# A hybrid attention and pooling block: W_out's quarter sums prepared early, loaded into attention's buffers, and later products begun inside the last heads

## The chip, the cores and the metric

The kernel is one launch on one core of a Trainium2 chip. A core has a matrix engine (PE, whose weight loads are listed apart as PEld), a vector engine (DVE), a scalar or activation engine (ACT), a general engine (POOL), and a sync engine (SP) whose queue issues every DMA of this kernel. The engines run side by side and wait for each other by semaphores; each executes its own instructions in the order in which the built program lists them. The metric is the time of the launch in microseconds; lower is better.

## The reference

The input x is 4096 tokens by 1024 channels, float32, with one conditioning vector c:

```python
mod = c @ w_ada + b_ada                      # 3072 numbers
shift, scale, gate = split(mod, 3)
h = rms_norm(x, norm_g) * (1 + scale) + shift
proj = h @ w_in                              # q|k|v|u|z: 512+512+512+512+1024
q, k = rms_norm(q, q_norm_g), rms_norm(k, k_norm_g)   # per head of 64
a_out = chunk_attention(q, k, v, rel_bias)   # 8 heads; a chunk of 64 tokens sees itself and 8 chunks to its left
p_out = multiscale_pool(u, w_pool, pool_scale)        # trailing means over 2, 4, 8, 16 frames
y = concat(a_out, p_out) * silu(z)
out = x + gate * (y @ w_out)                 # w_out is 1024 x 1024
```

## The kernel before

Every float32 product on PE is made of three matmuls: each operand is split into a rounded part `hi` and a rest `lo` (`split`, L101: ACT rounds, another engine subtracts), and hi·hi, hi·lo and lo·hi are summed in PSUM.

**The first stage** (pools `a_*`, L150 to L419) runs over eight groups of 512 tokens (`sg`). A group makes twelve products `n` of 24 matmuls each: gates of the pool half (`zp`), gates of the attention half (`za`), and the pooled channels `u`. Products with odd `n` go into one of two PSUM tiles `ps`, those with even `n` into one of four tiles `aps`, and `evac` (L325) empties them: for a gate ACT takes a sigmoid and DVE multiplies by the product. While a group runs, `load_x` fetches the next group's tokens, takes the root of their mean square, and sends it to DRAM and back as a row (`rs_d`, L200, and `rb`, L202); `prep` (L278) multiplies the transposed tokens by that row on POOL (L284), scales and shifts them on DVE (L285), and splits them. The normalised tokens are kept in `hT_d`, the gates in `gz_d`, the finished pool half of y in `yT_d`. At the end of the last group the 1024 numbers of `gate` are made (`ada`, eight times) and stored in `gate_d`.

**Attention** (L502 to L808) runs over 64 units: two passes of four heads, in each eight groups of 512 tokens, in each four heads. `s1_items` makes scores for one unit ahead (four blocks of 128 queries: PE, then DVE adds the bias and takes the extreme, then ACT takes the exponential); `s2_items` transposes the weights through PE and multiplies them by v. `proj_items` makes q, k and v of one block of 128 tokens for later units; its `evac_qk` squares q and k on POOL, sums on DVE, and takes eight reciprocal roots (`rsqrt`: three small DVE operations, then twelve small ones on POOL). `merge` interleaves these lists, and a scheduler that knows estimated durations then sets the final order of each engine's instructions.

**The output product** multiplies y (two blocks of 128 tokens at a time: block p and block p+16, p from 0 to 15, and the halves of the channels) by w_out with a scheme of seven block products per p. Two of the seven, w_out's two quarters in the first output half applied to block p, are `osteps`: 32 steps of 12 matmuls (`o_items`, L475). 24 of them (plan, L756) are handed to the units 58 to 63; the scheduler lays two more there. Their weights are loaded and split at u == 57 (`load_wo`). The other five products per p (`steps`, L850; called t = 2, 1, 3, 4, 0) use sums and differences of w_out's quarters. They begin when attention is over and its pools have been closed: `w_prep` (L833) loads w_out's quarters, forms the sums on DVE and POOL and splits them; `combine` (L864) forms sums and differences of y's blocks on POOL; `step` (L879) does 12 matmuls; the results are multiplied by `gate` on DVE and x is added on POOL (`finish`, L446).

Of the kernel before, what the change touches and what calls it, by code (L numbers as in the profile page):

```python
# [51 lines left out]
def block_kernel(ctx, tc, x, xT, par, crow, w_adaT, w_in, w_uT, bias, w_pool, w_out, rcnt, out):  # L52
# [17 lines left out]
    gate_d = dram.tile([1, D], F32, name="gate_d")  # L70
    s1_d = [dram.tile([P, SG], F32, name=f"s1_d{i}") for i in range(NPAIR)]
# [4 lines left out]
    nc.sync.dma_start(pt, par)  # L76

# [4 lines left out]
    def rsqrt(pool, src, n, inv_n, tag, eng=None):  # L82
# [3 lines left out]
        nc.vector.tensor_scalar(v, src, inv_n, EPS, op0=ALU.mult, op1=ALU.add)  # L86
# [63 lines left out]
    with ExitStack() as ca:  # L150
# [54 lines left out]
        mod = const.tile([P, 24], F32, name="mod")  # L205
        gcol = const.tile([P, KT], F32, name="gcol")
        psc = pt[:, C_PS : C_PS + 4]
        cb = wc.tile([P, D + 16], F32, name="cb")
        nc.gpsimd.memset(cb[:, D : D + 1], 1.0)

        def ada(pool, n):
            m = mod[:, n : n + 1]
            e = D if pool is xp else D + 1
            s_ = pool.tile([P, D if pool is xp else D + 16], F32, name="xt" if pool is xp else "w_s")[:, 0:e]
# [171 lines left out]
        nc.sync.dma_start(rc, rcnt)  # L386
        halo = [wc.tile([P, 16], F32, name=f"halo{g}") for g in range(4)]
# [3 lines left out]
        for sg in range(NSG):  # L391
            nxt = sg + 1 < NSG
            for n in range(12):
# [14 lines left out]
                evac(sg, n, ps)  # L408
                if not nxt and n == 3:
# [6 lines left out]
            if not nxt:  # L416
                for j in range(8):
                    ada(xp, 16 + j)
                nc.sync.dma_start(gate_d.rearrange("o (j p) -> p (o j)", p=P), mod[:, 16:24])  # L419


    op = ctx.enter_context(tc.tile_pool(name="b_qk", bufs=8))
    WO = {}
    gate = {}

    def load_wo(n, j, pool, stage):
        a_ = pool.tile([P, 2, 512], F32R, name="w")
        b_ = pool.tile([P, 2, 512], F32R, name="w")
        for t in range(2):
            s_ = stage()  # L430
            nc.sync.dma_start(s_, wo[:, 2 * j + t, n * 512 : n * 512 + 512])
            split(a_[:, t, :], b_[:, t, :], s_, nc.gpsimd)
            WO[n, 2 * j + t] = (a_[:, t, :], b_[:, t, :])
# [4 lines left out]

    def product(ps, a_, l_, W, start):
        for k in range(4):  # L440
            wh, wl = W[k]
            nc.tensor.matmul(ps, a_[:, k, :], wh, start=start and k == 0, stop=False, skip_group_check=True)  # L442
            nc.tensor.matmul(ps, a_[:, k, :], wl, start=False, stop=False, skip_group_check=True)  # L443
            nc.tensor.matmul(ps, l_[:, k, :], wh, start=False, stop=k == 3, skip_group_check=True)  # L444

    def finish(c, n, xr, b, eng):  # L446

        nc.vector.tensor_tensor(c, c, gate[n], op=ALU.mult)
        eng.tensor_tensor(c, c, xr, op=ALU.add)
        nc.sync.dma_start(out[b * P : (b + 1) * P, n * 512 : (n + 1) * 512], c)  # L450
# [13 lines left out]
    def o_load(i):  # L464
        if i < len(osteps):
# [9 lines left out]
    def o_items(i):  # L475
        half, p = osteps[i]

        def one(k):
# [4 lines left out]
            wh, wl = WO[0, half * 4 + k]  # L483
# [3 lines left out]
            if k == 3:  # L487
                OH.pop(i)
                o_load(i + 2)
                t = op.tile([P, 512], F32, name="qkr")  # L490
                if half == 0:
                    nc.scalar.copy(t, ps)
                    nc.sync.dma_start(s1_d[p], t)
                else:
                    nc.vector.tensor_tensor(t, ps, gate[0], op=ALU.mult)
                    nc.gpsimd.tensor_tensor(t, t, xr, op=ALU.add)
                    nc.sync.dma_start(out[p * P : (p + 1) * P, 0:512], t)
# [4 lines left out]
    with ExitStack() as cb:  # L502
# [21 lines left out]
        gqn = bp.tile([P, 1], F32, name="gqn")  # L524
# [19 lines left out]
        Vt, QK, QS, QL = {}, {}, {}, {}  # L544

        def proj_items(ph, b, after=None):
# [20 lines left out]
            def evac_qk(ps):  # L567
# [4 lines left out]
                ssq = st.tile([P, 8], F32, name="ssq")  # L572
                nc.vector.tensor_reduce(ssq, sq.rearrange("p (a b) -> p a b", b=HD), axis=AX.X, op=ALU.add)
                r = rsqrt(st, ssq, 8, 1.0 / HD, "rq", nc.gpsimd)
                r3 = raw.rearrange("p (a b) -> p a b", b=HD)
                nc.gpsimd.tensor_tensor(r3, r3, r.unsqueeze(2).broadcast_to([P, 8, HD]), op=ALU.mult)
                QK[ph, b] = raw

# [162 lines left out]

        units = [(ph, sg, h) for ph in range(2) for sg in range(NSG) for h in range(HP)]
# [13 lines left out]
        for i in range(24):  # L756
            plan[58 + i // 4].append(("o", i))
# [3 lines left out]
        def block_items(kb):  # L761
            if kb[0] == "o":
                return o_items(kb[1])
            it = proj_items(*kb, after=after.get(kb))
# [14 lines left out]
        for u in range(-1, 64):  # L779
# [21 lines left out]
            if u == 57:  # L801
                for n in range(2):
                    gate[n] = bp.tile([P, 512], F32, name=f"gate{n}")
                    nc.sync.dma_start(gate[n], gate_d[:, n * 512 : (n + 1) * 512].broadcast_to([P, 512]))
                for j in range(KT // 2):
                    load_wo(0, j, w1, stage)
                for j in range(2, 4):
                    load_wo(1, j, w1, stage)  # L808

    with ExitStack() as cd:  # L810
# [156 lines left out]
```

## Time and profile before

| | |
|---|---|
| runs | 1951.62, 1954.4, 1955.83 us; median 1954.4 |
| profiled execution | 1953.81 us, of which the span of the trace is 1952.0 |
| busy share | PE 97%, DVE 64%, POOL 49%, ACT 47% |
| matmuls | 10284 |
| DMA | 239.96 MB, mean 123 GB/s |

The page's table of 40 slices (48.8 us each) gives the busy share in tenths: PE stands at 9 or more in all but three of them (7 in the first, 6 and 7 in the 35th and 36th), and the granted clock of PE falls below 9 tenths only in the first, the 35th and the 36th. A matmul's listed duration overlaps that of the next, so pace is read from starts.

### The profile page before, as it was taken

How to read it: one execution, taken by the hardware profiler on the slowest of the kernel's cores; microseconds unless marked ns; L12 is line 12 of the kernel's file. 1: busy time of each engine (PE TensorE's matmuls, PEld its weight loads, DVE VectorE, ACT ScalarE, POOL GpSimd, SP SyncE). 2: the span in 40 equal slices, each digit the busy share in tenths (PEclk: the TensorE clock that was granted, in tenths of full speed). 3: DMA queues.
4: the chain of work that ended last, by engine and by line, in shares of the span. 5: the costliest groups of instructions: out<-in, count | busy, mean ns of one | idle time of the engine just before them, and what ended most of it. 6: DMA issues, size and time to landing. Idle time of an engine off the chain costs nothing. (4 is left out here: it accounts for less than half of the span.)

```text
span 1952.0 us, 30102 instructions
## 1 busy us (share of the span) xinstructions
PE 1890.8 (97%) x10284; PEld 1621.8 (83%) x10284; DVE 1247.7 (64%) x2456; ACT 913.4 (47%) x1951; POOL 948.3 (49%) x1449
## 2 busy tenths in 40 slices
PE   7999999999999999999999999999999999679998
PEld 6878888888888898898888888888898888568887
DVE  7664645464654557666676766657666654678896
ACT  4422212221324557656676666656666765422221
POOL 2431323132136653464565556544464654587774
PEclk8999999999999999999999999999999999889999
DMA  9654435434532222221233222112221455656664
GB/s 367 201 170 137 128 120 160 125 111 150 157 111 68 68 68 65 61 71 55 71 100 96 74 84 82 60 55 68 64 71 58 149 181 171 203 166 206 219 208 137
DMA packets 185066, 239.96 MB, mean 123 GB/s; under 512 B 20688, under 2 KB 96976, under 8 KB 184912
## 3 DMA queue, kind: packets, MB, share of 16 engines
q1 hardware_dynamic: 184912, 238.04, 38.1%
q8 instruction: 81, 1.33, 0.3%
q14 instruction: 73, 0.60, 0.1%
HBM read 166.53 MB, written 63.06 MB: 118 GB/s over the span
## 5 line engine op out<-in xcount | busy, mean ns | idle before, releaser
L556 PE MATMUL ps<-w,bhh 128*128 128x512 f32 (+1 forms) x1024 | 352.4, 344 | 0.3 <-ACT qkr L569 0.2
L557 PE MATMUL ps<-w,bhh 128*128 128x512 f32 (+1 forms) x1024 | 351.7, 343 | 0.0
L558 PE MATMUL ps<-w,bhl 128*128 128x512 f32 (+1 forms) x1024 | 350.9, 343 | 0.0
L699 DVE TENSOR_TENSOR ptl<-ptps,pth 128x512 fp32r<-128x512 f32 x480 | 224.1, 485 | 136.0 <-ACT pth L698 131.9
L103 POOL TENSOR_TENSOR bhl<-bhr,bhh 128x512 fp32r<-128x512 f32 x148 | 191.8, 1298 | 175.8 <-ACT bhh L102 157.2
L649 DVE CUSTOM_DVE_ANT_0 p<-sps,nb 128x640 f32<-128x640 f32 (+4 forms) x256 | 198.9, 777 | 115.7 <-PE sps L645 113.6
L662 ACT ACTIVATE p<-p,mx 128x640 f32<-128x640 f32 (+4 forms) x256 | 204.7, 800 | 101.7 <-DVE mx L649 100.6
L698 ACT CAST pth<-ptps 128x512 fp32r<-128x512 f32 x480 | 193.5, 426 | 124.2 <-PE ptps L692 111.8
L692 PE MATMUL ptps<-ident,p 128*128 128x128 f32 x1200 | 215.2, 275 | 1.6 <-ACT p L662 1.0
L556 PEld LDWEIGHTS ps<-w,bhh 128*128 128x128 f32 x1024 | 193.6, 189 | 18.2 <-DVE v L103 0.6
L558 PEld LDWEIGHTS ps<-w,bhl 128*128 128x128 f32 x1024 | 193.5, 189 | 17.7
L557 PEld LDWEIGHTS ps<-w,bhh 128*128 128x128 f32 x1024 | 193.6, 189 | 17.3
L710 PE MATMUL ops<-pth,v 128*128 128x512 f32 x480 | 162.1, 338 | 5.7 <-ACT pth L698 2.8
L692 PEld LDWEIGHTS ptps<-ident,p 128*128 128x128 f32 x1200 | 147.9, 141 | 21.1 <-ACT p L662 1.7
L644 PE MATMUL sps<-kr,qs 128*128 128x320 f32 (+2 forms) x480 | 154.8, 330 | 8.3 <-DVE mx L649 7.5
L711 PE MATMUL ops<-ptl,v 128*128 128x512 f32 x480 | 156.6, 335 | 2.9 <-DVE ptl L699 2.0
L322 PE MATMUL aps<-hlo,w 128*128 128x512 f32 x392 | 154.0, 393 | 0.0
L323 PE MATMUL aps<-hhi,w 128*128 128x512 f32 x392 | 152.5, 389 | 0.0
L321 PE MATMUL aps<-hhi,w 128*128 128x512 f32 x392 | 150.5, 394 | 0.0
L645 PE MATMUL sps<-kr,ql 128*128 128x320 f32 (+2 forms) x480 | 149.1, 319 | 0.0
L321 PE MATMUL ps<-hhi,w 128*128 128x512 f32 x376 | 147.5, 396 | 1.0 <-DVE gz L330 1.0
L322 PE MATMUL ps<-hlo,w 128*128 128x512 f32 x376 | 147.9, 393 | 0.0
(176 smaller groups left out, 4166.8 us busy)
## 6 DMA issues: line engine op xcount, KB each, us to landing
bhr<-hT_d SPq DMA_DIRECT2D x128, 256.0 KB
xt<-in_x_dram SPq DMA_DIRECT2D x32, 512.0 KB
qkr<-in_x_dram SPq DMA_DIRECT2D x64, 256.0 KB
dr<-yT_d SPq DMA_DIRECT2D x64, 256.0 KB
xt<-in_xT_dram SPq DMA_DIRECT2D x28, 512.0 KB
hT_d<-xt SPq DMA_DIRECT2D x56, 256.0 KB
w_s<-in_w_adaT_dram SPq DMA_DIRECT2D x16, 512.5 KB
gz_d<-gz SPq DMA_DIRECT2D x32, 256.0 KB
```

The source lines that it names most:

```text
L103: eng.tensor_tensor(lo, raw, hi.bitcast(F32), op=ALU.subtract)
L321: nc.tensor.matmul(ps, wh[:, cs], a_, start=k == 0, stop=False)
L322: nc.tensor.matmul(ps, wh[:, cs], l_, start=False, stop=False)
L556: nc.tensor.matmul(ps, a_, wh, start=k == 0, stop=False)
L557: nc.tensor.matmul(ps, a_, wl, start=False, stop=False)
L558: nc.tensor.matmul(ps, l_, wh, start=False, stop=k == KT - 1)
L649: nc.vector.tensor_tensor_reduce(out=p_[:, w0:WIN], in0=ps[:, s0 + w0 : s0 + WIN], in1=nb[ph, h][:, w0:WIN], scale=1.0, scalar=3e38, op0=A ...
L662: nc.scalar.activation(p_[:, w0:WIN], p_[:, w0:WIN], AF.Exp, scale=-1.0, bias=mx, accum_out=ls)
L692: nc.tensor.transpose(out=ps[:, i * P : (i + 1) * P], in_=Pt[ph, sg, h, i][:, w : w + P], identity=ident)
L698: nc.scalar.copy(a_[:, r], ps[:, r])
L699: nc.vector.tensor_tensor(l_[:, r], ps[:, r], a_[:, r].bitcast(F32), op=ALU.subtract)
L710: nc.tensor.matmul(o[:, r], v, a_[:, r], start=n == 0, stop=False, skip_group_check=True)
```

## The change

It has seven parts:

1. In the groups sg 1 and 2 of the first stage the eight parts of `gate` are made (`ada_gate`, in halves of 512 columns); `gate` then replaces c in the tile `cb`.
2. In the groups sg 3 to 6 `w_sums` loads w_out's quarters, multiplies them by `gate` on POOL, forms all the sums on POOL, splits them (ACT and DVE) and stores both parts in DRAM (`wg_d`: seven quarters of four k each).
3. `load_wo` loads such a quarter already split into the pool `w1`: the two quarters of the o-steps and that of t = 0 after unit 57, that of t = 1 when the last o-step of the first half is done, that of t = 4 when the last o-step is done. `w_head` loads those of t = 2 and t = 3 into the key, bias and query-rest tiles of a head, once that head's scores are over.
4. The pools of the last stage are gone: the results use attention's own tiles and PSUM.
5. All 32 o-steps and the first three of the 80 later steps are in the plan of the units 58 to 63.
6. `combine` and the additions to the results run on DVE; gate is no longer multiplied in, since the weights hold it; x is added straight from PSUM.
7. In `evac_qk` the roots of two blocks are taken together (16 numbers at once), and the first small operation of `rsqrt` runs on POOL.

```diff
-        nc.vector.tensor_scalar(v, src, inv_n, EPS, op0=ALU.mult, op1=ALU.add)
+        (eng or nc.vector).tensor_scalar(v, src, inv_n, EPS, op0=ALU.mult, op1=ALU.add)
...
+        def ada_gate(n):
+            acc = st.tile([P, 2], F32, name="acc")
+            for i in range(2):
+                s_ = a_stage()
+                nc.sync.dma_start(s_, w_adaT[n * P : (n + 1) * P, i * 512 : i * 512 + 512])
+                nc.vector.tensor_tensor_reduce(
+                    out=s_, in0=s_, in1=cb[:, i * 512 : i * 512 + 512], scale=1.0, scalar=0.0,
+                    op0=ALU.mult, op1=ALU.add, accum_out=acc[:, i : i + 1],
+                )
...
+        def w_sums(k):
+
+            g = nc.gpsimd
+            r = {}
+
+            def keep(q, raw):
+                hi = sh.tile([P, 512], F32R, name="bhr", tag="bhr", bufs=2)
+                lo = raw.bitcast(F32R)
+                split(hi, lo, raw, nc.vector)
+                nc.sync.dma_start(wg_d[q][k][:, 0, :], hi.bitcast(F32))
+                nc.sync.dma_start(wg_d[q][k][:, 1, :], raw)
+
+            for i, n in ((0, 0), (0, 1), (1, 1), (1, 0)):
+                r[i, n] = a_stage()
+                nc.sync.dma_start(r[i, n], wo[:, 4 * i + k, n * 512 : n * 512 + 512])
+                g.tensor_tensor(r[i, n], r[i, n], gb[:, n * 512 : n * 512 + 512], op=ALU.mult)
+            t1, t2 = a_stage(), a_stage()
+            g.tensor_tensor(t1, r[0, 1], r[0, 0], op=ALU.subtract)
+            keep(0, r[0, 0])
...
+                if sg in (1, 2) and 5 <= n < 9:
+                    ada_gate(12 + 4 * sg + n - 5)
...
+                if 3 <= sg < 7 and n == 5:
+                    w_sums(sg - 3)
...
-            if not nxt:
-                for j in range(8):
-                    ada(xp, 16 + j)
...
+    def load_wo(q, pool):
+
+        W = WO[q] = {}
+        for k in range(4):
+            t = pool.tile([P, 2, 512], F32R, name="w")
+            nc.sync.dma_start(t.bitcast(F32), wg_d[q][k])
+            W[k] = (t[:, 0, :], t[:, 1, :])
...
+                o = b % 2
+                if o == 0:
+                    SSQ[0] = st.tile([P, 16], F32, name="ssq")
...
+                if o == 0:
+                    return
+                r = rsqrt(st, ssq, 16, 1.0 / HD, "rq", nc.gpsimd)
...
+        def fetch_y(p):
+            for i, h, kind in ((1, 0, "p"), (1, 1, "p"), (0, 0, "p"), (0, 1, "v")):
+                b = p + i * NPAIR
+                raw = RAW[p, i, h] = spare(kind if p == 1 else "v")
+                nc.sync.dma_start(
+                    raw.rearrange("p (k t) -> p k t", k=4), yT_d[b // NB][b % NB, :, 4 * h : 4 * h + 4, :]
+                )
...
+                xr = XR[p, {2: 0, 1: 3}.get(t, t)]
+                nc.vector.tensor_tensor(xr, ps, xr, op=ALU.add)
+                if t in (2, 1, 4):
+                    nc.vector.tensor_tensor(xr, xr, SX[p], op=ALU.add)
...
+        def w_head(q, k0, h):
+
+            t = kp.tile([P, 2, 512], F32R, name="wkr", tag=f"kr{h}")
+            nc.sync.dma_start(t.bitcast(F32), wg_d[q][k0])
+            hi = bp.tile([P, WIN], F32R, name="wnb", tag=f"nb{h}")[:, 0:512]
+            lo = kp.tile([P, SG], F32R, name="wql", tag=f"ql{h}")
+            nc.sync.dma_start(hi.bitcast(F32), wg_d[q][k0 + 1][:, 0, :])
+            nc.sync.dma_start(lo.bitcast(F32), wg_d[q][k0 + 1][:, 1, :])
+            W = WO.setdefault(q, {})
+            W[k0], W[k0 + 1] = (t[:, 0, :], t[:, 1, :]), (hi, lo)
+
+        def o_done(i):
+            if osteps[i] == (0, NPAIR - 1):
+                load_wo(1, w1)
+            elif osteps[i] == (1, NPAIR - 1):
+                load_wo(4, w1)
...
-        for i in range(24):
-            plan[58 + i // 4].append(("o", i))
+        for u, n0, n1 in ((58, 0, 7), (59, 7, 14), (60, 14, 21), (61, 21, 28), (62, 28, 32)):
+            plan[u] += [("o", i) for i in range(n0, n1)]
+        plan[62].append(("d", 0))
+        plan[63] += [("d", 1), ("d", 2)]
...
-        def w_prep(k):
-            r = {}
-            for i in range(2):
-                for n in range(2):
-                    r[i, n] = dr.tile([P, 512], F32, name="dr")
-                    nc.sync.dma_start(r[i, n], wo[:, 4 * i + k, n * 512 : n * 512 + 512])
...
-        def combine(t, p):
-
-            g = nc.gpsimd
...
+            if u == 57:
+                for q in (0, 10, 11):
+                    load_wo(q, w1)
+            if u in (59, 60):
+                w_head(2, 2 * (u - 59), u - 59)
+            if u in (61, 62):
+                w_head(3, 2 * (u - 61), u - 59)
```

Where the order of instructions moves:

SP's queue of DMAs in the first stage, between the token loads of one group and the rest of the group's stores. Names: `xt` tokens, `rs_d` and `rb` the root's way to DRAM and back, `hT_d` normalised tokens, `wg_d_0_134` the first stored quarter (k = 0). Before:

```order
L280 DMA xt<-in_xT_dram 128x2x512 x3
L359 DMA yT_d_87<-gz 128x4x128
L280 DMA xt<-in_xT_dram 128x2x512
L200 DMA rs_d_97<-rxy 128x4x1
L202 DMA rb<-rs_d_97 128x512
L291 DMA hT_d_73<-xt 128x4x128 x8
```

and now:

```order
L422 DMA bhh<-in_w_out_dram 128x512 x2
L286 DMA xt<-in_xT_dram 128x2x512
L208 DMA rs_d_97<-rxy 128x4x1
L417 DMA wg_d_0_134<-bhr 128x512
L210 DMA rb<-rs_d_97 128x512
L418 DMA wg_d_0_134<-bhh 128x512
L417 DMA wg_d_0_154<-bhr 128x512
L417 DMA wg_d_0_142<-bhr 128x512
L418 DMA wg_d_0_154<-bhl 128x512
L418 DMA wg_d_0_142<-bhh 128x512
L297 DMA hT_d_73<-xt 128x4x128
```

A store of a rounded quarter now stands between `rs_d` and `rb`, and others ahead of the tokens' stores.

SP's queue at the end of attention. Names: `dr` and `w`, `wkr`, `wql`, `wnb` are tiles for w_out's quarters, `s_d_*` and `y` partial results and y. Before:

```order
L359 DMA yT_d_92<-osum 128x4x128
L670 DMA rl_d_7_1_132<-rt 8x32 x4
L676 DMA rlx<-rl_d_7_1_132 64x512 x2
L838 DMA dr<-in_w_out_dram 128x512 x3
L819 DMA gate_19506<-gate_d 128x512
L819 DMA gate_19508<-gate_d 128x512
L838 DMA dr<-in_w_out_dram 128x512 x5
```

and now:

```order
L484 DMA w<-wg_d_1_159 128x1024
L484 DMA w<-wg_d_2_160 128x1024
L484 DMA w<-wg_d_3_161 128x1024
L538 DMA out_dram<-qkr 128x512
L493 DMA qkr<-in_x_dram 128x512 x2
L882 DMA wkr<-wg_d_2_156 128x1024
L886 DMA wql<-wg_d_3_157 128x512
L885 DMA wnb<-wg_d_3_157 128x512
L808 DMA yp<-yT_d_89 128x512 x2
L808 DMA yp<-yT_d_85 128x512
L720 DMA rl_d_7_1_132<-rt 8x32 x4
```

The quarter of t = 4 (`w`) and the second half of that of t = 3 (`wkr`, `wql`, `wnb`) are now issued ahead of the last unit's own small transfers (`rl_d`).

DVE in the last stretch, one pair p. Names: `yps`, `zps` and `ps`, `ptps` are PSUM, `bhl` a rest, `qkr`, `s`, `u` results. Before:

```order
L895 TENSOR_TENSOR qkr<-yps,s_21016 128x512
L103 TENSOR_TENSOR bhl<-dr,bhh 128x512
L896 TENSOR_TENSOR qkr<-zps,qkr 128x512
L448 TENSOR_TENSOR qkr<-qkr,gate_19508 128x512
L892 TENSOR_TENSOR u_21196<-yps,s_21135 128x512
L103 TENSOR_TENSOR bhl<-dr,bhh 128x512
L899 TENSOR_TENSOR s_21016<-yps,s_21016 128x512
```

and now:

```order
L824 TENSOR_TENSOR yp<-yv 128x512
L830 TENSOR_TENSOR yv<-yv 128x512
L867 TENSOR_TENSOR qkr<-ps,qkr 128x512
L111 TENSOR_TENSOR bhl<-yv,bhh 128x512
L869 TENSOR_TENSOR qkr<-qkr,yp 128x512
L867 TENSOR_TENSOR qkr<-ptps,qkr 128x512
L111 TENSOR_TENSOR bhl<-yv,bhh 128x512
```

Before, a pair has 13 operations on DVE (five of L103, three of L448, and L892, L895, L896, L899, L902) and seven on POOL; now it has 17 on DVE (five each of L111 and L867, three of L869, and L824, L825, L830, L835) and none on POOL.

## Rows read from the trace of the kernel before

**Rows 1.** stages of attention and end: busy us (instructions), clock, DMA share, GB/s

```profile
core 0: us, PE busy (x) PEld busy (x) DVE busy (x) ACT busy (x) POOL busy (x), PEclk, DMA share, GB/s
560.00:1536.00 976.00, 961.07 (x6027) 852.66 (x6026) 626.84 (x1519) 597.48 (x1370) 541.79 (x1115) 1.00 0.24 74
1536.00:1546.00 10.00, 8.77 (x45) 7.75 (x46) 8.02 (x22) 9.08 (x24) 4.48 (x4) 0.83 0.45 137
1546.00:1662.00 116.00, 116.00 (x636) 99.45 (x635) 59.65 (x129) 70.61 (x151) 57.37 (x45) 1.00 0.53 175
1662.00:1678.00 16.00, 13.27 (x82) 10.75 (x80) 11.29 (x28) 10.74 (x27) 3.79 (x3) 1.00 0.17 53
1678.00:1741.00 63.00, 38.29 (x131) 29.75 (x132) 43.49 (x38) 16.73 (x30) 52.15 (x35) 0.78 0.66 221
1741.00:1941.00 200.00, 199.13 (x879) 164.62 (x877) 171.68 (x192) 45.55 (x73) 143.07 (x96) 1.00 0.61 199
```

**Rows 2.** PE's waits over the whole span: us in total, times, longest

```profile
PE ps L484 <- DVE qkr L495: 14.0, 3, 7.5
PE yps L442 <- ACT bhh L102: 10.9, 1, 10.9
PE sps L644 <- DVE mx L649: 7.5, 19, 1.1
...
PE ps L321 <- DVE gz L330: 1.0, 1, 1.0
```

**Rows 3.** PE in order of time, 1677 to 1745: start, us, instruction, idle before

```profile
1677.50 0.33 PE L711 MATMUL ops<-ptl,v 128*128 128x128 f32 x1
1685.31 0.80 PE L484 MATMUL ps<-w,bhh 128*128 128x512 f32 x1 [7.48 <-DVE qkr L495]
...
1725.88 0.80 PE L442 MATMUL yps<-w,bhh 128*128 128x512 f32 x1 [10.89 <-ACT bhh L102]
...
1729.84 0.40 PE L443 MATMUL yps<-w,bhh 128*128 128x512 f32 x1
...
1741.41 0.39 PE L442 MATMUL zps<-w,bhh 128*128 128x512 f32 x1
...
1744.81 0.39 PE L442 MATMUL zps<-w,bhh 128*128 128x512 f32 x1
```

**Rows 4.** SP in the first stage, timeline around 314 to 322 us

```profile
313.87 0.37 SPq L200 DMA_DIRECT2D rs_d<-rxy  x1
322.04 0.34 SPq L202 DMA_DIRECT2D rb<-rs_d  x1
```

**Rows 5.** POOL in the first stage, the same stretch

```profile
325.32 11.45 POOL L284 TENSOR_TENSOR xt<-xt,rb 128x512 f32<-128x512 f32 x8 [18.79 <-DMA rb<-rs_d]
```

**Rows 6.** DVE in the first stage, the same stretch

```profile
336.99 0.68 DVE L330 TENSOR_TENSOR gz<-gz,ps 128x512 f32<-128x512 f32 x1
```

**Rows 7.** ACT in the first stage, the same stretch

```profile
340.75 0.60 ACT L329 ACTIVATE gz<-aps 128x512 f32<-128x512 f32 x1 [4.89 <-PE aps L323]
```

**Rows 8.** DVE by line, 1741 to 1941: busy us, mean ns, idle before

```profile
L103 DVE TENSOR_TENSOR bhl<-dr,bhh 128x512 fp32r<-128x512 f32 x74 | 84.3, 1140 | 2.6 <-ACT bhh L102 2.6
L448 DVE TENSOR_TENSOR u<-u,gate 128x512 f32<-128x512 f32 x15 | 24.5, 1631 | 0.0
...
L895 DVE TENSOR_TENSOR qkr<-yps,s 128x512 f32<-128x512 f32 x15 | 10.4, 692 | 14.2 <-PE yps L444 14.2
...
L448 DVE TENSOR_TENSOR s<-s,gate 128x512 f32<-128x512 f32 x15 | 10.2, 678 | 0.0
```

**Rows 9.** all engines, the end of the timeline

```profile
1946.81 0.69 DVE L902 TENSOR_TENSOR u<-zps,u 128x512 f32<-128x512 f32 x1 [1.30 <-PE zps L444]
...
1948.98 0.33 SPq L450 DMA_DIRECT2D out_dram<-u  x1
```

**Rows 10.** DMA rate in 40 slices of 1678 to 1741

```profile
GB/s 185 299 134 235 362 401 382 400 349 267 221 131 213 407 398 265 291 247 372 90 0 333 31 307 170 242 294 121 166 43 124 0 30 303 0 12 164 294 338 202
```

**Rows 11.** small POOL and DVE operations of the roots, 560 to 1536

```profile
L91 POOL TENSOR_TENSOR rqw<-rqy 128x8 f32<-128x8 f32 x192 | 38.7, 202 | 44.9 <-DVE rqy L88 34.8
```

More of the change, by code (lines that the diff above doesn't have):

```diff
@@ L415, in block_kernel @@
                     load_wqkv(0, 1, lambda: a_stage(), nc.vector)
-            if not nxt:
-                for j in range(8):
-                    ada(xp, 16 + j)
-                nc.sync.dma_start(gate_d.rearrange("o (j p) -> p (o j)", p=P), mod[:, 16:24])
-    op = ctx.enter_context(tc.tile_pool(name="b_qk", bufs=8))
-    WO = {}
[L424 to L433, printed above, removed]
-    XP = {}
[L439 to L450, printed above, removed]
+    op = ctx.enter_context(tc.tile_pool(name="b_qk", bufs=9))
+    WO = {}
+    def load_wo(q, pool):
[4 more added lines that the diff above has]
+            W[k] = (t[:, 0, :], t[:, 1, :])
+    XP = {}
     def load_xr(b, n):
@@ L464, in o_load @@
     def o_load(i):
-        if i < len(osteps):
+        if i >= len(osteps):
+            combine(*steps[i - len(osteps)])
+        else:
             half, p = osteps[i]
@@ L740, in s2_items, with spare @@
             return seq
+        steps = [(2, 0)]
+        for p in range(NPAIR):
+            steps += [(1, p), (3, p)] + ([(2, p + 1)] if p + 1 < NPAIR else []) + [(4, p), (0, p)]
+        RAW, SX, XR, YP, ZP, DH = {}, {}, {}, {}, {}, {}
+        def spare(kind):
+            if kind == "v":
+                return vp.tile([P, 512], F32, name="yv", tag="v")
+            return sp.tile([P, WIN], F32, name="yp", tag="p")[:, 0:512]
+        def fetch_y(p):
[4 more added lines that the diff above has]
+                    raw.rearrange("p (k t) -> p k t", k=4), yT_d[b // NB][b % NB, :, 4 * h : 4 * h + 4, :]
+                )
@@ new lines, in d_items, with one @@
+        def d_items(i):
+            t, p = steps[i]
+            def one(k):
+                if k == 0:
+                    if t == 2:
+                        if p == 0:
+                            YP[p] = pp.tile([P, SG], F32, name="ps")
+                        else:
+                            YP[p] = ptp.tile([P, SG], F32, name="ptps")
+                            if p + 1 < NPAIR:
+                                fetch_y(p + 1)
+                                fetch_x(p + 1)
+                    if t == 1:
+                        ZP[p] = pp.tile([P, SG], F32, name="ps")
+                ps = ZP[p] if t in (1, 0) else YP[p]
+                a_, l_ = DH[t, p]
+                wh, wl = WO[11 if t == 0 else t][k]
+                start = t in (1, 2) and k == 0
+                nc.tensor.matmul(ps, a_[:, k, :], wh, start=start, stop=False, skip_group_check=True)
+                nc.tensor.matmul(ps, a_[:, k, :], wl, start=False, stop=False, skip_group_check=True)
+                nc.tensor.matmul(ps, l_[:, k, :], wh, start=False, stop=k == 3, skip_group_check=True)
+                if k < 3:
+                    return
+                xr = XR[p, {2: 0, 1: 3}.get(t, t)]
+                nc.vector.tensor_tensor(xr, ps, xr, op=ALU.add)
+                if t in (2, 1, 4):
+                    nc.vector.tensor_tensor(xr, xr, SX[p], op=ALU.add)
+                if t not in (2, 1):
+                    b = p if t == 0 else p + NPAIR
+                    n = 0 if t == 4 else 1
+                    nc.sync.dma_start(out[b * P : (b + 1) * P, n * 512 : (n + 1) * 512], xr)
+                if i + 2 < len(steps):
+                    combine(*steps[i + 2])
+            return [lambda k=k: one(k) for k in range(4)]
```

185 lines of the change are left out of this document (72 added, 113 removed).

## The prediction

> **What bounds the kernel now.** I read the table of slices first: PE is full nearly everywhere, so only stretches where it is not full, or at half clock, can be won. Then the stages [rows 1]: attention up to 1536 has PE idle for 15 of 976 us, the stretch of the heads that carry o-steps (1546 to 1662) for none, and in the last stretch (1741 to 1941) PE waits 0.9 us in 200. Between 1662 and 1741 it is idle for 2.7 and 24.7 us, the second time at a mean clock of 0.78. Third, PE's waits [rows 2]: the two longest entries, 14.0 us for DVE's additions to the o-steps and one wait of 10.9 us for the rounding of the first sum of y, both belong to that hole. Everything else is small: 7.5 us over 19 waits for DVE in attention, 1.0 us in the first stage. The changed kernel has as many matmuls as before, so the question is how much of the hole closes, and what the work moved ahead of it costs where it now stands.
>
> **What is removed.** Attention's last matmul starts at 1677.50 and takes 0.33, so it is over at 1677.83; the last stretch runs at full pace from 1729.84 [rows 3]. Between lie the six o-steps that the order of before puts behind attention (72 matmuls) and the first nine matmuls of the later steps, 81 in all. The pace at full clock is (1744.81 - 1741.41) / 15 = 0.2267 us per matmul [rows 3]. 81 need 18.4 us; 52.0 were spent. The hole is 33.6 us, its waits and its half clock together. Its causes go one by one: weights loaded and split on the spot, gate's broadcast, the pools' closing, sums of y on POOL. The last unit ran without filling work: 16 - 13.27 = 2.7 us [rows 1]; now three later steps lie in it. At 1536 to 1546, where the projections are used up and the o-steps have not begun, PE is idle for 1.2 us and runs at 0.83 of its clock, another 1.7: 2.9 [rows 1]; the new order puts its first o-steps there. At the very end three DVE operations on the last tile become one: from 1946.81 to the store's issue at 1948.98 is 2.17 us [rows 9], of which one operation (0.69 and some hundredths) stays: 1.5. Together 40.7 us.
>
> **What is added in the first stage.** In four groups, per group: four products and four subtractions on POOL, seven roundings on ACT, seven subtractions on DVE, four loads and fourteen stores of 256 KB; in two earlier groups eight half-row reductions on DVE. PE is never short of work there except for 1.0 us [rows 2], and the other engines have room. What can reach PE is an evacuation that comes late. Before, DVE finishes the gate of product n = 3 at 336.99 + 0.68 = 337.7 [rows 6], since it stands behind operations that wait for POOL, which waits for `rb` until 325.32 [rows 5]; `rb` is issued at 322.04, 8.2 us behind `rs_d` [rows 4]. Product n = 7 takes the same PSUM tile and starts when n = 6 ends and its activation begins, at 340.75 [rows 7]. The slack is 3.1 us. In the new order fewer token operations stand ahead of that gate on DVE, but four of the new subtractions do, and on ACT five roundings through two buffers. These cannot pass the stores that free the buffers. If a store takes x from issue to landing, the fifth rounding comes two landings after `rb`'s issue and the gate is out at about 325 + 2x. With x = 3.3, what `rb` itself took (322.04 to 325.32), that is 332, earlier than before; with 8.2, what `rs_d` took, it is 341, just late. I take 0.5 us for each of four groups, 2 us; the bounds are 0 and 12.
>
> **What is added in attention.** For two blocks, 24 small POOL operations of 0.2 us [rows 11] become 13, so POOL is freed by 11 x 0.2 x 32 = 70 us in all; it was not on the path. DVE drops two of three starting operations per pair and one more, but now waits once per pair for POOL's first one; queued behind it are the extremes and additions on which PE's scores wait. The gain is at most PE's 7.5 us of waits [rows 2]; the loss is at most about the same again if every pair costs 0.25 us. I take 0.
>
> **What is added in the last heads.** Their stretch now holds 35 steps instead of 26. From 1536 to 1678 it took 142 us; less 5.6 us found above and 312 matmuls (70.7) leaves 65.7 for attention; with 420 matmuls (95.2) it will take 161. In it, in sizes from the code: five stored quarters of 2.1 MB, four half quarters of 1.05, the o-steps' 21 MB, y and x of the first two pairs 4.2, attention's own 5 or so: 45 MB, 280 GB/s. Rows 1 show 175 GB/s at a share of 0.53 and 221 at 0.66, so some 335 GB/s at a full share, and single slices of the old hole reach 401 [rows 10]. On average this fits; in bursts it doesn't. When the last o-step ends there are still to come: some 1.3 MB of the quarter of t = 1, the 2.1 of t = 4, four blocks of 0.26, the last 1.05 of t = 3; 5.5 MB, or 16.4 us at 335 GB/s. PE wants that last half after t = 2, t = 1 and half of t = 3 (6.8 us) and the attention laid between (I estimate 5.5, somewhat under half of the last unit's 13.27 in rows 1): 12.3. So 4 us are lost there. Behind it come y's blocks for the second pair (0.8 MB, 2.4 us) and two additions, a rounding and a subtraction (2.7 us by rows 8 and 9), partly hidden: 3 us. At the start of the stretch 4.2 MB of weights stand ahead of the third o-step's y: 2 us. Sum 9; bounds 0 (at 401 GB/s the first wait is 1.4, and then nothing is late behind it) and 20 (at 221 GB/s it is 12.6). After waits of this length the rows show half clock; 1 us more, at most 4.
>
> The Trainium skill, "DMA: Bandwidth & Descriptors", Queues, rings and completion order, says that what SP issues is consumed in ring order on each DMA engine: a late small load can't pass the weights ahead of it. By that rule the three waits stand; were the transfers to share the rate, the half quarter would land early and the sum would be 9 us lower. No row here separates the two.
>
> **The last stretch.** DVE goes from 13 to 17 operations per pair, POOL from seven to none, PE needs 60 x 0.2267 = 13.6 us per pair. A PSUM addition takes 0.69 [rows 8]. Operations with both inputs in SBUF have means of 1.14 and 1.63 us, but 0.68 in the group of the tile `s` [rows 8], the same work at another moment of POOL's. With POOL silent I take 0.69 for all: 11.7 us, under 13.6, hidden. If the slow means were the operations' own, 5 x 1.14 + 5 x 0.69 + 7 x 1.1 = 16.9, and the pairs would be DVE's: rival D.
>
> The Trainium skill, "SBUF — State Buffer", SBUF: two separate sides, says that a DVE instruction with two SBUF inputs is held up by a POOL instruction that reads SBUF. By that rule all 17 take the short time; without it the sum would be about 50 us higher. Rows 8 agree (1.63 against 0.68), though they don't show POOL's part by themselves.
>
> **Sum.** 1953.8 (the profiled execution) - 40.7 + 2 + 0 + 9 + 1 = 1925. The median of the runs, 1954.4, is 0.6 above that execution, which changes nothing.
>
> **The rivals.** A, as above, 1918 to 1932: chance 0.48. B, the loads are always in time: 1953.8 - 40.7 + 0 to 4, near 1915 (1910 to 1918): 0.20. For it: the average rate fits, and the scheduler placed the steps; against it: half of the weights come in bursts. C, the hole moves into the heads: weights late at the start and at the end, the rate near 221 GB/s, each wait followed by half clock; 20 to 33 us of stalls, 1936 to 1950, middle 1941: 0.19. For it: the old hole itself, where loads at 221 GB/s left PE at 38 us of 63 [rows 1]. D, the pairs are bound by DVE: 15 x (16.9 - 13.6) = 50 us, 1975: 0.03, as rows 8 speak against it. E, slower by the first stage: stores landing later than 12 us. The gate is then late by 325 + 2x - 340.75, four times; with x = 14 that is 49 us, 1972; it decides over the whole gain from x = 12, and costs anything only from x = 8. 0.05. F, the scheduled change does not reach the path: the o-steps stay waiting for weights as long as before, within 4 us of 1954: 0.05.
>
> **Range and chances.** From 1911 to 1948 lie A, nearly all of B and most of C: 0.8. A measurement of this kernel tells 0.2% (4 us) from no change. Faster by more than that, under 1950.5: A, B and C, 0.87 less a little of C's upper end: 0.86; within it 0.06; slower 0.08, D and E.
>
> **What would show it.** Right: PE's share in the 40 slices stays at 9 to the end; no wait over 5 us behind attention; the waits that are left name DMA or the roundings of y behind it, near the last unit; DVE's operations of the last stretch at 0.69; the first stage's groups as far apart as before. Wrong: a wait of PE for an evacuation of `ps` in the groups 3 to 6 (E), waits for DVE in every pair (D), half clock in the last four units (C). The forecast fails on its main term if PE still loses more than 15 us between 1536 and the full pace of the last stretch.

## The result, and the profile after

The changed kernel takes 1918.5 us (median of four runs, 1917.2 to 1920.2) against 1954.4 (1951.6 to 1955.8) for the kernel before: ratio 0.9819, interval 0.9802 to 0.9836. The forecast was 1925, range 1911 to 1948. The profiled execution took 1920.2 us, 1.7 above the median, with a span of 1918.4 (1952.0 before); what follows is in spans.

Two points cut the program into pieces with equal work: the first and the last start of the projections' first matmul, which the view by source line gives. Before and after:

```profile
L556 PE MATMUL ps<-w,bhh x1024: 274/386/502, 565.8 to 1528.4; 128*128 128x256 f32 x86, 128*128 128x512 f32 x85
```

```profile
L596 PE MATMUL ps<-w,bhh x1024: 274/387/506, 559.7 to 1527.8; 128*128 128x512 f32 x86, 128*128 128x256 f32 x85
```

| piece | before | after | change | forecast |
|---|---|---|---|---|
| first stage, to the first projection | 565.8 | 559.7 | -6.1 | +2 |
| attention with projections | 962.6 | 968.1 | +5.5 | 0 |
| from the last projection to the end | 423.6 | 390.6 | -33.0 | -40.7 + 9 + 1 = -30.7 |

The three changes add up to -33.6, the forecast's to -28.7. The total came out so near partly by luck: the misses in the first two pieces, 8.1 us too fast and 5.5 too slow, nearly cancel. The stages after, with the columns of [rows 1]:

```profile
core 0: us, PE busy (x) PEld busy (x) DVE busy (x) ACT busy (x) POOL busy (x), PEclk, DMA share, GB/s
240.00:540.00 300.00, 300.00 (x1326) 248.46 (x1325) 180.50 (x267) 91.46 (x159) 112.20 (x94) 1.00 0.58 189
560.00:1528.00 968.00, 952.04 (x5960) 844.82 (x5959) 580.15 (x1371) 588.50 (x1351) 466.29 (x749) 1.00 0.25 75
1528.00:1538.00 10.00, 9.01 (x57) 7.25 (x56) 8.66 (x23) 8.29 (x21) 4.38 (x8) 1.00 1.02 405
1538.00:1655.00 117.00, 117.00 (x641) 100.70 (x640) 63.47 (x135) 69.58 (x149) 39.73 (x31) 1.00 0.63 207
1655.00:1677.00 22.00, 20.50 (x109) 17.25 (x108) 11.56 (x23) 11.48 (x26) 7.75 (x6) 1.00 0.73 258
1677.00:1716.00 39.00, 33.44 (x162) 26.94 (x161) 28.09 (x52) 12.94 (x29) 2.90 (x2) 0.96 0.89 318
1716.00:1910.00 194.00, 194.00 (x857) 160.62 (x856) 150.40 (x237) 43.62 (x70) 0.00 (x0) 1.00 0.57 184
```

The hole of 63 us at 0.61 busy and a mean clock of 0.78 [rows 1] has become one stretch of 39 us with 5.6 idle, at 0.96. Added up over the stages behind the projections, PE's idle time falls from 29.5 us [rows 1] to 8.1, which is 21.5 of the 33.0 us gained there; most of the rest is time at half clock that is gone. The bubble where the projections end has kept 1.0 of its 1.2 idle us, but at full clock. The undisturbed pace has no part in it: behind the last projection matmuls of 512 columns that start within 0.26 us of each other have a mean distance of 0.2277 us before and 0.2278 after. PE's waits, to be held against [rows 2]:

```profile
PE sps L694 <- DVE mx L699: 6.9, 22, 0.9
...
PE ops L760 <- ACT pth L748: 3.5, 7, 1.4
PE ops L761 <- DVE ptl L749: 2.5, 4, 0.9
PE ps L860 <- DVE qkr L867: 2.4, 1, 2.4
```

The two long entries of before, 14.0 and 10.9 us, are gone. The 2.4 us is the longest wait left behind attention. DVE in order of time shows what it is:

```profile
1708.94 0.69 DVE L824 TENSOR_TENSOR yp<-yv 128x512 f32<-128x512 f32 x1 [1.41 <-DMA yv<-yT_d]
1709.55 0.68 DVE L869 TENSOR_TENSOR qkr<-qkr,yp 128x512 f32<-128x512 f32 x1
1710.15 0.68 DVE L867 TENSOR_TENSOR qkr<-ps,qkr 128x512 f32<-128x512 f32 x1
```

The sum for a later pair (L824) waits for its y, and the addition that frees PE's bank (L867) stands two places behind it in DVE's order. PE, from its last matmul ahead of the wait:

```profile
1708.10 0.39 PE L861 MATMUL ptps<-wkr,bhh 128*128 128x512 f32 x1
1710.89 0.50 PE L860 MATMUL ps<-w,bhh 128*128 128x512 f32 x1 [2.40 <-DVE qkr L867]
...
1712.14 0.63 PE L861 MATMUL ps<-w,bhh 128*128 128x512 f32 x1
...
1715.34 0.40 PE L860 MATMUL ptps<-wkr,bhh 128*128 128x512 f32 x1
```

0.63 us in place of 0.39 are matmuls at half clock; together they cost some 1.7 us. DVE by line in the last stretch, for [rows 8]:

```profile
L867 DVE TENSOR_TENSOR qkr<-ptps,qkr 128x512 f32<-128x512 f32 x42 | 29.0, 690 | 31.5 <-PE ptps L862 31.4
L111 DVE TENSOR_TENSOR bhl<-yv,bhh 128x512 fp32r<-128x512 f32 x42 | 28.7, 682 | 0.0
...
L824 DVE TENSOR_TENSOR yp<-yv 128x512 f32<-128x512 f32 x12 | 8.3, 690 | 0.4
```

All of DVE's operations take 0.69 us, as forecast, and PE is busy throughout.

### The profile page after: what moved, and what is told of

Read it like the earlier page. It is cut to its first block, busy times and chain, and to the rows that moved or that the text cites. A ratio compares the mean times of both kernels' runs of the same rounds, so it can differ in the third digit from the quotient of the medians.

```text
span 1918.4 us, 29756 instructions
## 1 busy us (share of the span) xinstructions
PE 1879.5 (98%) x10284; PEld 1617.8 (84%) x10284; DVE 1199.4 (63%) x2414; ACT 913.8 (48%) x1951; POOL 707.9 (37%) x979
## 4 chain that ended last, share of the span: by engine, by line
PE 86%; DVE 5%; DMA 3%; issue 2%; ACT 2%; POOL 1%; SPq 0%; ACTq 0%; POOLq 0%; DVEq 0%
PE ps L596 9%; PE ps L597 9%; PE ps L598 9%; PE ptps L742 5%; PE aps L327 4%; PE aps L328 4%; PE aps L329 4%; PE ps L327 4%; PE ps L328 4%; PE ps L329 4%; PE sps L694 3%; PE ops L761 3%; PE sps L695 3%; PE ops L760 3%; PE ptps L862 2%
## 5 line engine op out<-in xcount | busy, mean ns | idle before, releaser
L749 DVE TENSOR_TENSOR ptl<-ptps,pth 128x512 fp32r<-128x512 f32 x480 | 223.1, 484 | 154.2 <-ACT pth L748 150.1
L111 POOL TENSOR_TENSOR bhl<-bhr,bhh 128x512 fp32r<-128x512 f32 x148 | 190.8, 1292 | 156.8 <-ACT bhh L110 123.2
L611 POOL TENSOR_TENSOR sq<-qkr 128x512 f32<-128x512 f32 x64 | 67.0, 1046 | 247.9 <-ACT qkr L609 239.3
```

What stands on the lines that cost most here:

```text
L749: nc.vector.tensor_tensor(l_[:, r], ps[:, r], a_[:, r].bitcast(F32), op=ALU.subtract)
```

## The experiments

Twelve kernels ran, four at a time with the kernel before on the same chip. The length of a stretch (566 to 1528 and so on) is read from one execution of each kernel; how far it scatters, a repeat of the changed program (d_late, below) shows: 966.8 us in attention against 968.1, and 388.4 from the last projection to the end against 390.6.

### Why the first stage became 5 us faster: place_off, place_on, shift_both, apart_256

The prediction passed over three lines of the change: an unused constant tile of 8 columns, the constants `mod`, `gcol` and `gqn` in front of the weights, and 128 spare columns in the row tile `cb` instead of 16. They move the tiles in SBUF. In the first stage PE is busy all the time in both kernels, yet in the same 300 us it starts 1326 matmuls after and 1313 before:

```profile
240.00:540.00 300.00, 300.00 (x1313) 246.14 (x1312) 158.29 (x258) 73.44 (x127) 69.92 (x65) 1.00 0.44 138
```

The mean distance of their starts, without gaps, is 0.2267 against 0.2289 us. The edits of place_off, place_on (on the kernel before), shift_both and apart_256 (the comments are added here; where `cb` changes in the changed kernel, a scratch tile of the same width changes with it):

```diff
-    const.tile([P, 8], F32, name="fill")
+    const.tile([P, 24], F32, name="fill")          # place_off, shift_both
-        cb = wc.tile([P, D + 128], F32, name="cb")
+        cb = wc.tile([P, D + 16], F32, name="cb")  # place_off; D + 64 in apart_256
...
+    const.tile([P, 16], F32, name="fill")          # place_on, in the kernel before
-        cb = wc.tile([P, D + 16], F32, name="cb")
+        cb = wc.tile([P, D + 32], F32, name="cb")  # place_on
```

> The changed kernel with its tiles of the first stage put back where the kernel before had them: the unused constant tile is 24 columns instead of 8 and the row tile has 16 spare columns instead of 128, so that the stationary weights lie 64 bytes behind a multiple of 128 and the moving tiles on a multiple. Nothing is computed otherwise. Theory P, the place of the tiles sets the pace of the first stage's matmuls: the spacing of their starts goes from 0.2267 back to 0.2289 us, 2304 x 0.0022 = 5 us, so near 1923.6. Rival Q, the pace comes from something else in the change or differs from execution to execution: the spacing stays at 0.2267 and the time at 1918.5 within 1.

> The kernel before with one part of the change alone: an unused constant tile of 16 columns and 16 more spare columns in the row tile, so that all operands of the first stage's matmuls lie on multiples of 128 bytes. Theory P: the spacing of the first stage's matmuls falls from 0.2289 to 0.2267 us and the first stage ends 5 us earlier, 1949.3. Rival Q: 0.2289 and 1954.4 as before.

> The changed kernel with everything behind the constants moved by 64 bytes: stationary weights and moving tiles of the first stage both lie 64 bytes behind a multiple of 512. So far the spacing of the first stage's matmuls was 0.2267 us with weights and moving tiles the same distance behind a multiple of 512 (0 and 0), 0.2289 with 64 bytes between the two (448 and 0; 64 and 128) and 0.2324 with 128 between them (0 and 128). Theory D, the distance between the two decides: 0.2267, first stage over at 560, time 1918.5. Rival M, each has to lie on a multiple of 512: 0.2289 or more, 5 us or more longer, 1923.5 or more.

> The changed kernel with 64 spare columns in the row tile instead of 128: the moving tiles lie 256 bytes behind a multiple of 512, the weights on one. Theory D1, the spacing grows with the distance (0.2267, 0.2289, 0.2324 at 0, 64, 128): at 256 near 0.239, 2304 x 0.0125 = 28 us, 1947. Rival D2, only offsets that are not a multiple of 256 cost: 0.2267 and 1918.5.

Places are bytes behind a multiple of 512, from the built program; the last column is the count of the row 240 to 540:

| kernel | weights | moving tiles | spacing, us | time, us | matmuls in 300 us |
|---|---|---|---|---|---|
| before | 448 | 0 | 0.2289 | 1954.4 | 1313 |
| place_off | 64 | 128 | 0.2289 | 1922.6 | 1312 |
| place_on | 0 | 128 | 0.2324 | 1960.4 | 1293 |
| changed | 0 | 0 | 0.2267 | 1918.5 | 1326 |
| shift_both | 64 | 64 | 0.2267 | 1919.5 | 1326 |
| apart_256 | 0 | 256 | 0.2267 | 1917.9 | 1325 |

The slowest and the shifted one, as the same row of each:

```profile
240.00:540.00 300.00, 300.00 (x1293) 243.21 (x1292) 158.41 (x259) 72.81 (x125) 69.75 (x66) 1.00 0.45 137
```

```profile
240.00:540.00 300.00, 300.00 (x1326) 248.47 (x1325) 179.94 (x267) 92.09 (x159) 109.04 (x94) 1.00 0.58 189
```

place_off loses the pace and 4.1 us (ratio 0.9840, 0.9826 to 0.9854), and its first stage ends at 565.0 instead of 559.7: the change's own work has nothing to do with it. place_on refuted the first form of the theory: with both operands on multiples of 128 it became 6.6 us slower than before (1.0033, 1.0021 to 1.0044). What orders all six is the distance of weights and moving tile: 0 and 256 bytes give 0.2267, 64 gives 0.2289 (0 - 448 is 64 too, modulo 512), 128 gives 0.2324. That the two need not lie on multiples of 512 is shown by shift_both. It fits that in the last stretch of the kernel before weights and split y both lie at 448, and the spacing there is 0.2267 [rows 3]. Other distances weren't tried, and why the distance counts stays open.

### What the roots in pairs cost: single, pairs

```diff
-                o = b % 2
...
-                r = rsqrt(st, ssq, 16, 1.0 / HD, "rq", nc.gpsimd)
-                for m in range(2):
...
+                r = rsqrt(st, ssq, 8, 1.0 / HD, "rq", nc.gpsimd)
```

(single, in the changed kernel; pairs is the reverse in the kernel before. The first operation of the root goes to DVE or POOL with it.)

> The changed kernel with the roots of attention taken block by block again, the first operation on DVE as in the kernel before. Theory R, the roots in pairs are what made attention's stretch with projections (5958 matmuls) 5.5 us longer: it goes from 968.1 back to 963 to 965 us, and the time to 1914 to 1916. Rival S, the 5.5 us are a half-clock stretch and the order of the scheduler, not the roots: the stretch stays at 967 to 969 and the time at 1918.5 within 1.

> The kernel before with the roots of attention in pairs alone (and one more buffer for the rows that wait for their partner). Theory R: attention's stretch of 5958 matmuls goes from 962.6 to 966 to 968 us and the time from 1954.4 to 1958 to 1960. Rival S: no change, 962 to 964 and 1954.4 within 1.

```profile
L596 PE MATMUL ps<-w,bhh x1024: 274/378/500, 560.8 to 1525.3; 128*128 128x512 f32 x86, 128*128 128x256 f32 x85
```

```profile
L556 PE MATMUL ps<-w,bhh x1024: 277/386/504, 565.3 to 1530.4; 128*128 128x512 f32 x86, 128*128 128x256 f32 x85
```

The first is single: attention 964.5 us and 1914.9 in all (0.9799, 0.9786 to 0.9811). The second is pairs: 965.1, 2.5 more than before, while the whole time (1954.5, ratio 1.0001, 0.9992 to 1.0010) can't tell it from nothing. Taken over all the profiles, ten with pairs have 965.1 to 968.1 us in attention (mean 966.5), and four without (before, place_on, single, best) 962.4 to 964.5 (mean 963.2). So the pairs lose 2 to 4 us in attention; it is seen in the stretch, and in the total only as a tendency. Of the 5.5 us of the profiled execution another 1.7 is a half-clock stretch behind two waits for DVE (0.93 and 0.81 us), which doesn't come in the repeat, d_late:

```profile
735.00:739.00 4.00, 3.77 (x14) 3.31 (x15) 2.83 (x6) 2.08 (x5) 1.44 (x2) 0.57 0.57 164
```

By which instruction the pairs lose it was not isolated.

### How near the first stage is to its limit: w_twice

```diff
-                if 3 <= sg < 7 and n == 5:
+                if 3 <= sg < 7 and n in (5, 9):
                     w_sums(sg - 3)
```

> The changed kernel with the quarter sums of the output weights made, split and stored twice in each of the four groups (the second time the same numbers into the same places). Theory W0, they cost the first stage nothing: PE has 0.1 us of idle time in it, and other engines have room: spacing 0.2267, first stage over at 559.7, time 1918.5 within 1.5. Rival W1, the forecast's 0.5 us per group: 2 us more, 1920.5. Rival E, the stores hold back the roundings and with them an evacuation: PE waits for an evacuation in each group, 12 us or more in all, 1930 or more.

1954.7 us, 36 more, in the range of rival E but not by its wait. The second set stands between product n = 9 and the next group's tokens, and these come late:

```profile
PE aps L328 <- DVE hlo L111: 17.1, 4, 4.6
PE aps L327 <- ACT hhi L110: 8.6, 4, 3.2
```

```profile
299.00:372.00 73.00, 68.00 (x287) 55.44 (x286) 47.95 (x67) 23.34 (x42) 37.05 (x31) 0.95 0.73 239
372.00:448.00 76.00, 69.32 (x293) 56.55 (x292) 50.02 (x68) 23.43 (x42) 39.17 (x33) 0.93 0.73 239
```

The four groups behind such a pair of sets take 74 to 77 us each instead of 65, with 5 to 8 idle and half clock on top, though DVE is busy for only 48 to 50 of them. In one such group:

```profile
367.96 0.62 ACT L110 CAST bhr<-bhh 128x512 fp32r<-128x512 f32 x1 [2.80 <-DMA wg_d<-bhr]
368.62 0.69 DVE L111 TENSOR_TENSOR bhh<-bhh,bhr 128x512 fp32r<-128x512 f32 x1 [2.30 <-ACT bhr L110]
...
380.20 0.68 DVE L111 TENSOR_TENSOR hlo<-xt,hhi 128x512 fp32r<-128x512 f32 x1
```

ACT's rounding waits for a store that frees its buffer, DVE's subtraction waits for the rounding, and the tokens' rest (`hlo`), on which PE waits until 380.93, stands behind them and the sums of `u` in DVE's order. So one set is free and a second one at that place costs 9 us. The idle time ahead of the subtractions speaks for the order of the queues rather than the load, but a second set at another place was not tried. The stores do hold back the roundings, as rival E says; what comes late are split tokens, not an evacuation.

### Whether the handover needs later steps in the last unit: d_late, d_after

d_late takes the three later steps out of the plan; d_after gives the first pair's sum the PSUM bank of attention's own sums:

```diff
-        plan[62].append(("d", 0))
-        plan[63] += [("d", 1), ("d", 2)]
...
-        for i in range(3, len(steps)):
+        for i in range(len(steps)):
```

```diff
                         if p == 0:
-                            YP[p] = pp.tile([P, SG], F32, name="ps")
+                            YP[p] = pop.tile([P, SG], F32, name="ops")
```

> The changed kernel with no later product inside the last units of attention: all 80 steps stand behind it, so the last unit has no filling work but what the scheduler pulls in. Theory L, the forecast's term: 2.7 us more, 1921. Rival L0, the scheduler draws the steps into the last unit anyway, since they wait for nothing else: same time within 1. Rival L2, the weights and y have more time to land behind attention and what is lost in the last unit comes back: 1916 to 1918. Rival L3, the longer waits of PE bring half clock as in the kernel before: 6 us or more, 1925 or more.

> The changed kernel with the first pair's sum of the products 2, 3 and 4 in the PSUM bank that attention's own sums use: these products can begin only when attention's last sum is out. By the written order one later step is left between attention's last matmuls, instead of three and more. Theory L, the forecast's term: the last unit runs with too little filling work, some 2 us more, 1920.5. Rival L2, what is lost in the last unit comes back behind it, since weights and y have more time: 1918.5 within 1. Rival L3, longer waits bring half clock as in the kernel before: 6 us or more, 1924.5 or more.

d_late came out with every engine's order unchanged: the scheduler draws the steps into the last unit whatever the plan says. It is therefore a repeat: 1918.0 us (0.9812, 0.9797 to 0.9827). d_after does move them, and takes 1915.3 (0.9808, 0.9793 to 0.9823), no loss that can be told. Its waits:

```profile
1685.33 0.44 PE L742 MATMUL ptps<-ident,p 128*128 128x128 f32 x2 [1.19 <-ACT p L712]
1695.06 0.79 PE L860 MATMUL ops<-w,bhh 128*128 128x512 f32 x1 [2.73 <-DVE yv L835]
```

One wait of 2.7 us for a sum of y has taken the place of the changed kernel's 2.40 and smaller ones, as rival L2 says. The later steps in the last unit are not worth their 2.7 us by themselves; what they gain there is lost to late y behind it.

### Late y or late weights: y_first

```diff
+            if u == 62:
+                fetch_y(1)
             if u in (61, 62):
                 w_head(3, 2 * (u - 61), u - 59)
...
-            if u == 62:
-                fetch_y(1)
```

> The changed kernel with the loads of y for the second pair ahead of the last half of t = 3's weights, not behind it; in the written order they now stand behind the first of its three loads (512 KB) and ahead of the two others (256 KB each). Theory Y, the loads are used up in the order in which they were issued: y of the second pair lands 1.5 us earlier (0.5 MB at 335 GB/s), DVE's wait for it (1.7 us) goes, and PE's two waits for DVE behind it (0.9 and 0.4) become shorter; 1 to 2 us less, 1917. Rival Y0, the transfers share the rate or y has to wait for the next pairs' loads anyway: 1918.5 within 1. Rival Y2, the weights are late in place of y: 1920 or more.

```profile
1696.30 0.39 PE L761 MATMUL ops<-ptl,v 128*128 128x256 f32 x1 [0.30 <-DVE ptl L749]
1697.96 0.44 PE L761 MATMUL ops<-ptl,v 128*128 128x384 f32 x1 [0.23 <-DVE ptl L749]
1707.82 0.50 PE L860 MATMUL ps<-w,bhh 128*128 128x512 f32 x1 [0.47 <-DVE qkr L867]
```

In the changed kernel the same three waits are 0.43, 0.89 and 2.40 (0.78, 0.89 and 1.23 in d_late, and one of 1.20 behind them); two small ones, of 0.33 and 0.59, follow here. PE waits for none of the weights that now stand behind y. The waits are those that theory Y names; the total, 1916.7 (0.9817, 0.9802 to 0.9832), can't tell 1 to 2 us. The issue of y's loads and the first sum that waits for them, behind the same operation of attention on DVE, in the changed kernel and here:

```profile
1690.17 1.38 SPq L808 DMA_DIRECT2D yp<-yT_d  x3
1692.15 1.75 DVE L749 TENSOR_TENSOR ptl<-ptps,pth 128x512 fp32r<-128x512 f32 x3 [0.58 <-ACT pth L748]
1695.57 0.69 DVE L824 TENSOR_TENSOR yv<-yp 128x512 f32<-128x512 f32 x1 [1.67 <-DMA yp<-yT_d]
```

```profile
1687.68 1.38 SPq L808 DMA_DIRECT2D yp<-yT_d  x3
1690.62 1.75 DVE L749 TENSOR_TENSOR ptl<-ptps,pth 128x512 fp32r<-128x512 f32 x3 [0.58 <-ACT pth L748]
1692.94 0.69 DVE L824 TENSOR_TENSOR yv<-yp 128x512 f32<-128x512 f32 x1 [0.57 <-DMA yp<-yT_d]
```

Measured from L749 y lands 1.1 us earlier (theory Y: 1.5), and its issue alone comes 1.0 us earlier; from issue to use it takes 5.4 and 5.3 us. So the gain can come from the earlier issue alone. The Trainium skill, "DMA: Bandwidth & Descriptors", Queues, rings and completion order, has descriptors consumed in ring order on each DMA engine; this run doesn't decide between that and a shared rate.

### POOL beside DVE in the last stretch: pool_sums

```diff
         def combine(t, p):
-            g = nc.vector
+            g = nc.gpsimd
```

> The changed kernel with the sums of y (four operations per pair of tiles, both inputs in SBUF) on POOL again, as in the kernel before; nothing else is moved. In the changed kernel POOL is silent in the last stretch and DVE's operations with two SBUF inputs take 0.68 us. Theory V, POOL's reading is what slowed them before: with POOL at work again the subtraction of the splits and the additions to the rows rise from 0.68 to 1.0 us or more, with the shape, line and data of each unchanged; four sums per pair leave DVE meanwhile, so that PE is still not kept waiting: 1918.5 within 3. Rival V0, the long durations were those operations' own: 0.68 stays, and the time is 1918.5 within 1. Rival V2, slower operations and POOL's longer chain in front of each product make PE wait in each pair: 1930 or more.

1916.6 us (0.9814, 0.9799 to 0.9829): PE is not kept waiting. More than that, the waits for DVE behind attention (0.43, 0.89 and 2.40) are gone but for 0.15, and one of 0.73 for ACT has come: the sums that wait for y no longer stand in DVE's order ahead of what frees PE's banks. In one pair, in order of time:

```profile
1801.82 1.29 POOL L835 TENSOR_TENSOR yv<-yv,yp 128x512 f32<-128x512 f32 x1
1801.87 0.69 DVE L867 TENSOR_TENSOR qkr<-ptps,qkr 128x512 f32<-128x512 f32 x1 [1.28 <-PE ptps L862]
1802.48 1.18 DVE L111 TENSOR_TENSOR bhl<-yv,bhh 128x512 fp32r<-128x512 f32 x1
...
1804.79 0.68 DVE L111 TENSOR_TENSOR bhl<-yp,bhh 128x512 fp32r<-128x512 f32 x1
```

The same subtraction takes 0.68 alone and 1.18 when POOL's sum is under way; it ends 0.55 behind POOL's end (1801.82 + 1.29 = 1803.11; 1802.48 + 1.18 = 1803.66). The addition from PSUM, beside the same POOL operation, keeps 0.69. Over the stretch L111 from `yv` has a mean of 0.986; the subtractions that meet no POOL operation keep 0.68. The Trainium skill, "SBUF — State Buffer", SBUF: two separate sides, calls it a lock held for the whole instruction; the trace agrees. The rise for the additions to the rows is smaller (0.684 to 0.785) than expected.

### All together: best

Single roots, y first, and this:

```diff
-                if t in (2, 1, 4):
+                if t in (2, 1):
                     nc.vector.tensor_tensor(xr, xr, SX[p], op=ALU.add)
+                if t == 1:
+                    nc.vector.tensor_tensor(XR[p, 4], XR[p, 4], SX[p], op=ALU.add)
```

> The changed kernel with attention's roots block by block, y of the second pair ahead of the last weights, and the stored sum added to the fourth quarter's rows one product earlier, so that one operation stands between the last matmul and the last store instead of two. From the run with single roots (1914.9): 0.6 less for the operation at the end, 0 to 2 less for y: 1912 to 1914.5.

1928.5 us, 14 more than single. Attention is the shortest of all (962.4), but the moved addition reads a tile of x that has not landed, and DVE holds everything behind it:

```profile
1772.36 0.69 DVE L861 TENSOR_TENSOR qkr<-qkr,yp 128x512 f32<-128x512 f32 x1 [4.34 <-DMA qkr<-in_x_dram]
1772.97 0.68 DVE L857 TENSOR_TENSOR qkr<-ptps,qkr 128x512 f32<-128x512 f32 x1
```

```profile
PE ptps L850 <- DVE qkr L857: 14.4, 12, 2.5
```

L857 frees the bank for which PE waits, in 12 of the pairs. Without that edit the two other parts were not run together; single (1914.9) is the best kernel by its ratio, d_after lies within its interval.

## Why the prediction was right, and where it was not

- **The hole** (33.6 us, with the other removals 40.7). Right in mechanism and nearly in size: from the last projection to the end 33.0 us went, against 30.7. That the waits for weights, gate and first sums are gone is read from the traces; which of the change's parts closes how much of the hole was not separated by a run. The test that was named, no more than 15 us of PE's time lost from the end of the projections to full pace, is met: 1.0 + 1.5 + 5.6 idle and some 1.7 of half clock. Two other signs are met in part: the 36th slice of the 40 stands at 8, not 9 (in the kernel before the 40th too, besides the three named ahead of the prediction, is under 9: it stands at 8), and the waits that are left name DVE, which waits for y, not DMA or a rounding.
- **Late loads, 9 us, and 1 of clock.** This term was too large. PE never waits for weights in this execution (in shift_both once, 0.28 us): between the last o-step and the second half of t = 3 the scheduler laid more of attention than the 5.5 us of the estimate (attention's sums run on to 1706), and at the start 405 GB/s were moved, not 335. What is late is y, as the third part of that term said: 0.43 + 0.89 + 2.40 = 3.7 us of PE's waits, and 1.7 of half clock; y_first shortens the waits, and pool_sums all but ends them. The other 1.8 of the 5.6 us are waits for ACT.
- **The end of the kernel, 1.5 us.** Half of it came. The last step is one of t = 4, with two operations on DVE, not t = 0 with one:

```profile
1913.67 0.69 DVE L867 TENSOR_TENSOR qkr<-ptps,qkr 128x512 f32<-128x512 f32 x1 [2.03 <-DMA out_dram<-qkr]
1914.40 0.69 DVE L869 TENSOR_TENSOR qkr<-qkr,yp 128x512 f32<-128x512 f32 x1
```

(The profile names a store as what L867 waited for; PE's last matmul ends at 1913.64.) From L867's start to the end of L869 that is 1.42 us, where the three operations took 2.17 to the store's issue [rows 9]: 0.7 gained.

- **The first stage, +2.** This step failed: -6.1. The new work costs nothing where it stands (PE idle 0 in the row 240 to 540), so the slack was judged rightly, but the matmuls' own pace rose by 0.0022 us, 2304 times: 5 us from the padding, which the prediction left out. The rest, about 1 us, is two waits of 1.0 us each, in the first two groups, that the changed kernel's profile lacks, less a longer half clock and 0.5 us more waiting at the start; none of this was tested.
- **Attention's roots, 0.** Failed: the freed 70 us of POOL were off the path, as said, and the pairs cost 2 to 4 us, where the prediction let gain and loss cancel.
- **The last stretch, 0.69 for all of DVE's operations.** Right; pool_sums shows the reason.
- **The rivals.** B (loads always in time) is nearest by the size of the waits for weights, A by the wait for y. C and F don't occur. D is excluded by the last stretch. E doesn't occur; w_twice finds a cliff one set of sums away, with E's late roundings but with another wait of PE.

## What to carry to other kernels

Read a diff's paddings and unused tiles as part of the change, and when PE is fully busy compare how many matmuls it starts in equal windows: a pace can change where no wait does. Ahead of an operation that frees a PSUM bank, put nothing on the same engine that waits for a transfer: an addition moved "earlier" cost 14 us here (best), and moving the sums of y off DVE took away most of the waits that were left (pool_sums). And look at what a scheduler made of a written order before valuing it: three planned steps changed nothing.

## What was not expected of the hardware

The distance in SBUF between stationary and moving tile sets the pace of float32r matmuls of 512 columns: 0.2267 us at 0 and 256 bytes (behind multiples of 512), 0.2289 at 64, 0.2324 at 128, with PE busy throughout, in six kernels; no other distances were tried. A second set of sums brought 36 us where the first was free, with DVE busy for two thirds of the time.
